# Spreading a per-head reciprocal over partitions through DRAM inside a delta-rule recurrence

## The chip, the cores and the metric

The kernel runs on one core of a Trainium2 chip. The metric is device time in microseconds (us), the median of several runs; before the change it is 1085.88 us (three runs, 1084.61 to 1088.7). Engines: TensorE (PE, with its weight loads as PEld), VectorE (DVE), ScalarE (ACT), GpSimd (POOL) and SyncE (SP), which here only issues DMAs.

## The reference

One layer of a decoder trunk for a sequence of 512 positions and a width of 2048, in float32. After an RMSNorm, one projection gives the streams of two groups. Sixteen heads of 64 channels run a generalised delta rule:

```python
kk = (k * k_k[i]).astype(f32).reshape(B, T, N_HEADS, HEAD_SIZE)
kk = kk / jnp.maximum(jnp.linalg.norm(kk, axis=-1, keepdims=True), KK_EPS)
k = k * (1.0 + (a - 1.0) * k_a[i])
...
sa = jnp.einsum('bhvk,bhk->bhv', S, -kk_t)
S = (S * w_t[:, :, None, :]
     + sa[..., None] * (kk_t * a_t)[:, :, None, :]
     + v_t[..., None] * k_t[:, :, None, :])
y_t = jnp.einsum('bhvk,bhk->bhv', S, r_t)
...
y = head_group_norm(y, ln_w[i], ln_b[i])
bonus = jnp.sum(rh * kh * r_k[i].astype(f32), axis=-1, keepdims=True) * vh
y_rwkv = (y + bonus.reshape(B, T, D_RWKV)).astype(dt) * jax.nn.silu(g_rwkv)
```

The other group takes trailing-window means of 1024 channels. Both are multiplied by gates, projected by w_out and added to x; a gated per-layer embedding and a final RMSNorm follow. What matters here is the second line: the key is divided by its norm, one number for each head and position.

## The kernel before, in words

Channels lie on partitions, time on the free axis. Two reference heads share the 128 partitions, so there are eight "heads" j of 128 channels and 512 positions; each runs as eight chunks of 64 positions. Big products are made from float32 split into a rounded part and a remainder (`wsplit`, `split`: a cast on ScalarE, a subtraction on VectorE), three matmuls for each product.

The middle of the kernel, some 640 us, is a software pipeline over the heads. The order of TensorE's instructions is the order in which they are written (`keep_in_program_order`). A generator `big` holds the stream of large projection matmuls (zk, zr, zv, zg of the coming heads, zb of the pool group), and `pump(n)` puts n of them between two steps of a head, so that TensorE has work while the other engines answer. Weights of that stream come by SP's queue (`raw`, 4 buffers), are cast on ScalarE (`whi`) and split on VectorE (`wlo`). The order on the other engines is found by a list scheduler; `issue_after` puts one instruction behind another on its engine. Every engine, and SP's queue of DMAs, works in the order that results.

Names of a head's steps, in their order of time:

- `prepare_key`: kk = (k k_k)^2 on ScalarE, split into kqh and kql. `norm_key`: two matmuls with a block of ones, `blk`, sum kk over the 64 channels of a head and leave the sum on every partition (PSUM tile pss); a maximum with 1e-24 on VectorE writes it to kk. `scale_key`: reciprocal of kk (128x512, though a column holds only two different numbers), then times k and k_k.
- `decay_and_rate`: decay and rate from small low-rank products.
- `prepare`: the operands ar and bk of the score matmuls; kk enters bk's last product (line 600). Then kp for the bonus.
- `scores`: pm = bk x ar, 32 matmuls, then pbo for the bonus bv.
- `invert`: an inverse of 32x32 triangles by 31 steps on VectorE, spread over the chunks of the head before; the result goes through DRAM (xd) into x1.
- `gather`: y1, two transposes of x1 on VectorE; pq, pmv and px, small matmuls; before them `prepare_key`, `decay_and_rate`, `norm_key` and `scale_key` of the next head.
- `recur`: eight chunks; in each py reads the state, zs is formed on VectorE, pu solves, ScalarE copies to uv, ps updates the state sbd on VectorE. At its end the output ysb is normalised: statistics, and eight scalings of 128x64 (line 866).
- `finish`: transposes of ysb, then yo = scaled output, plus bv, times the gate sg (lines 877, 878), stored by a DMA of ScalarE's queue.

The loop runs `prepare(j + 1)`, `recur(j)` (in it, after the first chunk, `scores(j + 1)` and the steps of `invert(j + 1)`), `gather(j + 1)`. So the key of head j + 2 is normalised in `gather(j + 1)`, and what follows waits for it in `prepare(j + 2)`.

Of the kernel before, what the change touches and what calls it, by code (L numbers as in the profile page):

```python
# [9 lines left out]
F32 = mybir.dt.float32  # L10
# [3 lines left out]
ALU = mybir.AluOpType  # L14

P = 128
T = 512
# [4 lines left out]
NJ = DR // P  # L22
# [12 lines left out]
def trunk_kernel(ctx: ExitStack, tc: tile.TileContext, x, p, norm_g, w_in, mu, w0, w_up, a0, a_up,  # L35
                 k_k, k_a, r_k, ln_w, ln_b, w_pool, pool_scale, w_out, w_ple, w_pg, b_pg, final_g, out):
    nc = tc.nc
    PSUM = bass.MemoryType.PSUM
    x, p, w_in, w_out, w_ple, w_pg = x[0], p[0, 0], w_in[0], w_out[0], w_ple[0], w_pg[0]
    out = out[0]  # L40
# [79 lines left out]
    def dp(o, i):  # L120
        return dprm[:, o + i:o + i + 1]
# [370 lines left out]
    def pump(n):  # L492
        debt[0] += n
        while debt[0] > 0:
            c = next(big, None)
            if c is None:
                debt[0] = 0
                return
            debt[0] -= c
# [12 lines left out]
                assert (nm, j) in zt  # L512
        return zt[nm, j]

    pws, kks, late = {}, {}, [None]

    H1, H2, H3, H4, H5, HE = 6, 12, 20, 8, 13, 40

# [44 lines left out]
    def norm_key(j):  # L563
        kk, kqh, kql = kks[j]
        ps = psM.tile([P, T], F32, name=f"pss{j}", tag="m")
        mm(ps, blk, kqh, start=True, stop=False)
        mm(ps, blk, kql, start=False, stop=True)
        late[0] = nc.vector.tensor_scalar(kk, ps, 1e-24, None, ALU.max)

    def scale_key(j):  # L570
        k_, kk = need("k", j), kks[j][0]
        nc.vector.reciprocal(kk, kk)
        nc.vector.scalar_tensor_tensor(kk, k_, pc("k_k", j), kk, ALU.mult, ALU.mult)
        kks[j] = kk


    def prepare(j):
        k_, r_, v_ = need("k", j), need("r", j), need("v", j)
        pw, ipw, tha = pws.pop(j)
        kk = kks.pop(j)  # L580
        if j + 1 < NJ:
            load_ab(j + 1)


        ar = rw.tile([P, NCH // 2, 4, C], F32, name=f"ar{j}", tag="ar", bufs=2)
        bk = rw.tile([P, NCH // 2, 4, C], F32, name=f"bk{j}", tag="bk")
        k4 = kk.rearrange("p (q c t) -> p q c t", c=2, t=C)
        pw4 = pw.rearrange("p (q c) t -> p q c t", c=2)
        i4 = ipw.rearrange("p (q c) t -> p q c t", c=2)
        kp = rw.tile([P, T], F32, name=f"kp{j}", tag="kp")  # L590
        nc.vector.tensor_scalar(kp, tha, dp(33, j), dp(41, j), ALU.mult, ALU.add)
        nc.vector.tensor_tensor(kp, kp, k_, ALU.mult)
        nc.vector.tensor_scalar(tha, tha, 0.5, 0.5, ALU.mult, ALU.add)
        nc.vector.tensor_tensor(ar[:, :, 0::3, :], r_.rearrange("p (q c t) -> p q c t", c=2, t=C),
                                pw4[:, :, :, 1:C + 1], ALU.mult)
        nc.vector.tensor_tensor(bk[:, :, 0::3, :], kp.rearrange("p (q c t) -> p q c t", c=2, t=C), i4, ALU.mult)
        nc.vector.scalar_tensor_tensor(ar[:, :, 1:3, :], k_.rearrange("p (q c t) -> p q c t", c=2, t=C), dp(89, j),
                                       pw4[:, :, :, 0:C], ALU.mult, ALU.mult)
        nc.vector.tensor_tensor(kk, kk, tha, ALU.mult)
        nc.vector.tensor_tensor(bk[:, :, 1:3, :], k4, i4, ALU.mult)  # L600
        nc.vector.scalar_tensor_tensor(kp, r_, dp(49, j), kp, ALU.mult, ALU.mult)
        kph = rw.tile([P, T], F32R, name=f"kph{j}", tag="t", bufs=4)
        kpl = rw.tile([P, T], F32R, name=f"kpl{j}", tag="t", bufs=4)
        split(kph, kpl, kp)

        bkd = dram.tile([P, NCH * P], F32, name=f"bkd{j}", tag="bkd")
        nc.sync.dma_start(out=bkd, in_=bk.rearrange("p q s c -> p (q s c)"))
        st_[j] = dict(pw=pw, ar=ar, bk=bk, bkd=bkd, v_=v_, kp=(kph, kpl))
# [55 lines left out]
    def invert(j):  # L664
        nb = st_[j].pop("nb")
        xw = rw.tile([P, 8, 32], F32, name=f"xw{j}", tag="xw")
        tm = rw.tile([P, 8, 32], F32, name=f"tm{j}", tag="tm")
        for s in range(31):
            n_, w_ = s // 4 + 1, 31 - s
            xin = i32 if s == 0 else xw  # L670
            nc.vector.tensor_tensor(tm[:, 0:n_, 0:w_], xin[:, 0:n_, s:s + 1].to_broadcast([P, n_, w_]),
                                    nb[s // 16][:, s % 16:s % 16 + 1, s + 1:32].to_broadcast([P, n_, w_]), ALU.mult)
            if s == 0:
                nc.gpsimd.tensor_copy(xw, i32)
            nc.vector.tensor_tensor(xw[:, 0:n_, s + 1:32], xw[:, 0:n_, s + 1:32], tm[:, 0:n_, 0:w_], ALU.add)  # L675
            yield
        xd = dram.tile([2, 2, 8, 8, 4, 32], F32, name=f"xd{j}", tag="xd")
        for q in range(4):
            nc.sync.dma_start(out=xd[:, :, :, :, q, :].rearrange("a b u i c -> (a b u) i c"),
                              in_=xw[32 * q:32 * q + 32])  # L680
        x1 = rw.tile([P, 8, C], F32, name=f"x1{j}", tag="x1", bufs=2)
        nc.gpsimd.memset(x1, 0.0)
        for par in range(2):
            pb = 64 * (1 - par)
            for b in range(2):
                nc.sync.dma_start(out=x1[pb + 32 * b:pb + 32 * b + 32, :, 32 * b:32 * b + 32],
                                  in_=xd[par, b].rearrange("u i q c -> (i q) u c"))

        st_[j]["x1"] = x1


    def gather(j):
        d = st_[j]
        v_, mt = d.pop("v_"), d["mt"]
        if j + 1 < NJ:
            prepare_key(j + 1)
            decay_and_rate(j + 1)

        uv = rw.tile([P, NCH, P], F32, name=f"uv{j}", tag="uv")
# [11 lines left out]
        pump(H4)  # L711

        d.update(uv=uv)
        if j + 1 < NJ:
            norm_key(j + 1)
        pump(H5)
        pump(HX)

# [6 lines left out]

        y1 = rw.tile([P, 8, 32], F32, name=f"y1{j}", tag="tm")

        with tc.issue_after(late[0].ins):
            yt = [nc.vector.transpose(y1[pb:pb + 32], x1[pb:pb + 32, :, 0:32]) for pb in (0, 64)]
        if j + 1 < NJ:  # L730
            with tc.issue_after(yt[0].ins), tc.issue_after(yt[1].ins), tc.issue_after((normed or yt)[-1].ins):
                scale_key(j + 1)
        ps3 = psM.tile([P, 8, 32], F32, name=f"pq2{j}", tag="m")
        units(lambda u, par, pb: mm(ps3[pb + 32:pb + 64, u, :],
# [20 lines left out]
        d["mv"] = mv  # L755
        pump(H1)
        if pending:
            pending.pop()()
        pump(H1)


    def recur(j, work, between):
# [17 lines left out]
        for ch in range(NCH):  # L780
# [27 lines left out]
                    nc.scalar.copy(uv[pb:pb + 64, ch, hc], psu[hc, hc])  # L808
            step()
            pump(HC2)  # L810
            if ch < NCH - 1:
                pss = psS.tile([P, T], F32, name=f"ps{j}_{ch}", tag="s")
                mm(pss[:, 0:P], bkn[:, ch, :], uv[:, ch, :], start=True, stop=True)
                for h in range(2):
                    hc = slice(64 * h, 64 * h + 64)
                    with tc.high_priority(offset=HP):
                        if ch == 0:
                            lead[0] = nc.vector.tensor_scalar(nxt[hc, hc], pss[hc, hc], pcc[hc], None, ALU.mult)
                        else:
                            lead[0] = nc.vector.scalar_tensor_tensor(nxt[hc, hc], pss[hc, hc], pcc[hc], s0p[hc, :],  # L820
                                                                     ALU.mult, ALU.add)
                s0p = rw.tile([P, C], F32, name=f"s0p{j}_{ch}", tag="s0p", bufs=2)
                pcn = pw[:, ch + 1, C:C + 1]
                if ch < NCH - 2:
                    for h in range(2):
                        hc = slice(64 * h, 64 * h + 64)
                        nc.gpsimd.tensor_scalar(s0p[hc, :], nxt[hc, hc], pcn[hc], None, ALU.mult)  # L827
            if ch == NCH - 1:
                for c0 in range(0, NCH, 4):
# [10 lines left out]
                    for pr in range(2):  # L840
                        yr = slice(64 * pr, 64 * pr + 64)
                        nc.scalar.copy(ysb[yr, c0 // 2:c0 // 2 + 2, :], py4[yr, pr::2, :])
            step()
            if ch == 0:
                between()
            else:
                pump(HC3)
# [14 lines left out]
        nc.vector.tensor_scalar(ve8, mvr[:, :, 1:2], 64e-5, None, ALU.add)  # L862
        nt8 = rw.tile([P, 8, 1], F32, name=f"nt8{j}", tag="nt8")
        rsqrt(rs8, ve8, nt8)
        for i in range(8):
            last = nc.vector.tensor_scalar(y8[:, i, :], y8[:, i, :], mvr[:, i, 0:1], rs8[:, i, :],
                                           ALU.subtract, ALU.mult)
        normed.append(last)

        def finish():  # L870
            sg = need("g", j)
            ps = psM.tile([P, T], F32, name=f"pyt{j}", tag="m")
            for tt in range(NT):
                tr(ps[:, tt * P:(tt + 1) * P], ysb[:, tt, :], ident)
            yo = rw.tile([P, T], F32, name=f"yo{j}", tag="t", bufs=4)
            nc.scalar.activation(yo, ps, AF.Identity, scale=dp(57, j), bias=dp(65, j))
            nc.vector.tensor_tensor(yo, yo, bv, ALU.add)
            nc.vector.tensor_tensor(yo, yo, sg, ALU.mult)
            nc.scalar.dma_start(out=yd[j], in_=yo)

        pending.append(finish)

    HC, HT, HX = (6, 9, 9), 130, 13
    HS, HN = 5, 2
    HP = 1000
    pending, normed = [], []
    need("k", 0)
    need("r", 0)
    prepare_key(0)
# [11 lines left out]
    for j in range(NJ):  # L901
# [10 lines left out]
                                    in_=p[256 * h:256 * h + 256, :].rearrange("(t p) q -> p t q", p=P))  # L912
        if j + 1 < NJ:
            prepare(j + 1)
        recur(j, invert(j + 1) if j + 1 < NJ else iter(()), between)
        if j + 1 < NJ:
            gather(j + 1)
    pump(HE)
    pending.pop()()
    s2a.close()  # L920
    psB = ctx.enter_context(tc.tile_pool(name="psB", bufs=3, space=PSUM))
    lp = ctx.enter_context(tc.tile_pool(name="lp", bufs=1))
# [271 lines left out]
```

## Time and profile before

| what | value |
|---|---|
| median of three runs | 1085.88 us (1084.61 to 1088.7) |
| the profiled execution, whole | 1087.06 us |
| its span, first to last instruction | 1085.3 us |
| TensorE busy, weight loads | 97%, 80% |
| VectorE, ScalarE, GpSimd busy | 66%, 41%, 7% |
| mean granted TensorE clock | 0.996 of full |
| DMA, mean | 135 GB/s |

Busy shares are means over a start of some 50 us, the heads up to about 715 us, the output projection to about 910 us and the embedding gate. Matmuls overlap in the records, so that TensorE can show as busy while its next instruction starts a little late; the start times tell more than the busy time.

### The profile page before, as it was taken

How to read it: one execution, taken by the hardware profiler on the slowest of the kernel's cores; microseconds unless marked ns; L12 is line 12 of the kernel's file. 1: busy time of each engine (PE TensorE's matmuls, PEld its weight loads, DVE VectorE, ACT ScalarE, POOL GpSimd, SP SyncE). 2: the span in 40 equal slices, each digit the busy share in tenths (PEclk: the TensorE clock that was granted, in tenths of full speed). 3: DMA queues.
4: the chain of work that ended last, by engine and by line, in shares of the span. 5: the costliest groups of instructions: out<-in, count | busy, mean ns of one | idle time of the engine just before them, and what ended most of it. 6: DMA issues, size and time to landing. Idle time of an engine off the chain costs nothing.

```text
span 1085.3 us, 17105 instructions
## 1 busy us (share of the span) xinstructions
PE 1057.8 (97%) x5996; PEld 873.7 (80%) x5996; DVE 714.9 (66%) x1851; ACT 441.3 (41%) x901; POOL 70.9 (7%) x180
## 2 busy tenths in 40 slices
PE   5999999999999999999999999999999999999996
PEld 4888878888888887887888788888888888888885
DVE  6676968878779779688887966464432424445366
ACT  7633535335336244353353344543222222333337
POOL 2100010010110100100101101000000000000000
PEclk9999999999999999999999999999999999999999
DMA  7444443442533533433435343774434428354534
GB/s 234 112 120 113 135 115 86 114 123 74 156 93 110 143 95 100 117 87 107 115 95 152 99 127 104 244 238 152 166 126 142 168 97 263 129 180 150 178 99 156
DMA packets 212916, 146.94 MB, mean 135 GB/s; under 512 B 68085, under 2 KB 173150, under 8 KB 212830
## 3 DMA queue, kind: packets, MB, share of 16 engines
q1 hardware_dynamic: 192126, 112.28, 35.9%
q10 hardware_dynamic: 20704, 33.56, 9.5%
q8 instruction: 47, 0.77, 0.3%
q14 instruction: 39, 0.32, 0.1%
HBM read 122.21 MB, written 23.07 MB: 134 GB/s over the span
## 4 chain that ended last, share of the span: by engine, by line
PE 76%; DVE 4%; DMA 1%; ACT 1%; issue 0%; SPq 0%; ACTq 0%; DVEq 0%
PE acc_o L157 16%; PE acc_g L157 16%; PE zb L157 13%; PE zg L157 5%; PE zv L157 5%; PE zr L157 5%; PE zk L157 4%; PE pple L157 2%; PE py L157 2%; PE pu L157 1%; PE pm L157 1%; DMA n<-nd 1%; PE pp L157 1%; PE ps L157 1%; PE pmv L157 1%; PE px L1015 1%
## 5 line engine op out<-in xcount | busy, mean ns | idle before, releaser
L133 DVE TENSOR_TENSOR wlo_g<-raw_g,whi_g 128x512 fp32r<-128x512 f32 x84 | 57.1, 685 | 76.0 <-ACT whi_g L132 76.0
L157 PE MATMUL zb<-hhi,whi_b 128*128 128x512 f32 x256 | 106.0, 414 | 0.0
L133 DVE TENSOR_TENSOR wlo_o<-raw_o,whi_o 128x512 fp32r<-128x512 f32 x64 | 43.9, 690 | 91.4 <-ACT whi_o L132 91.4
L157 PE MATMUL zb<-hhi,wlo_b 128*128 128x512 f32 x256 | 100.4, 392 | 0.0
L157 PE MATMUL acc_o<-whi_o,ylo 128*128 128x512 f32 x256 | 100.2, 391 | 0.0
L157 PE MATMUL acc_o<-whi_o,yhi 128*128 128x512 f32 x256 | 99.9, 390 | 0.0
L157 PE MATMUL zb<-hlo,whi_b 128*128 128x512 f32 x256 | 99.8, 390 | 0.0
L157 PE MATMUL acc_o<-wlo_o,yhi 128*128 128x512 f32 x256 | 99.7, 390 | 0.0
L132 ACT CAST whi_g<-raw_g 128x512 fp32r<-128x512 f32 x84 | 52.0, 621 | 106.4 <-PE acc_g L157 59.4
L157 PE MATMUL acc_g<-whi_g,x2hi 128*128 128x512 f32 x208 | 81.2, 391 | 0.0
L157 PE MATMUL acc_g<-wlo_g,x2hi 128*128 128x512 f32 x208 | 81.0, 389 | 0.0
L157 PE MATMUL acc_g<-whi_g,x2lo 128*128 128x512 f32 x208 | 80.6, 389 | 0.0
L132 ACT CAST whi_o<-raw_o 128x512 fp32r<-128x512 f32 x64 | 39.9, 623 | 97.0 <-PE acc_o L157 96.7
L827 POOL TENSOR_SCALAR s0p<-sbd,pw 64x64 f32<-64x64 f32 x96 | 54.5, 568 | 338.6 <-DVE sbd L820 251.0
L132 ACT CAST whi_b<-raw_b 128x512 fp32r<-128x512 f32 x64 | 39.7, 621 | 85.4 <-PE zb L157 28.8
L133 DVE TENSOR_TENSOR wlo_b<-raw_b,whi_b 128x512 fp32r<-128x512 f32 x64 | 43.7, 684 | 28.0 <-ACT whi_b L132 27.6
L157 PEld LDWEIGHTS zb<-hhi,wlo_b 128*128 128x128 f32 x256 | 48.0, 188 | 10.9
L675 DVE TENSOR_TENSOR xw<-xw,tm 128x60 f32<-128x60 f32 (+24 forms) x248 | 52.1, 210 | 7.0
L157 PEld LDWEIGHTS acc_o<-wlo_o,yhi 128*128 128x128 f32 x256 | 48.1, 188 | 10.0
L157 PEld LDWEIGHTS acc_o<-whi_o,ylo 128*128 128x128 f32 x256 | 48.1, 188 | 9.8
L157 PEld LDWEIGHTS acc_o<-whi_o,yhi 128*128 128x128 f32 x256 | 48.1, 188 | 9.7
L157 PEld LDWEIGHTS zb<-hhi,whi_b 128*128 128x128 f32 x256 | 48.2, 188 | 8.3
(283 smaller groups left out, 2532.0 us busy)
## 6 DMA issues: line engine op xcount, KB each, us to landing
raw_b<-in_w_in_dram SPq DMA_DIRECT2D x64, 256.0 KB
raw_o<-in_w_out_dram SPq DMA_DIRECT2D x64, 256.0 KB
raw_g<-in_w_pg_dram SPq DMA_DIRECT2D x64, 256.0 KB
raw_k<-in_w_in_dram SPq DMA_DIRECT2D x32, 256.0 KB
raw_r<-in_w_in_dram SPq DMA_DIRECT2D x32, 256.0 KB
raw_v<-in_w_in_dram SPq DMA_DIRECT2D x32, 256.0 KB
raw_g<-in_w_in_dram SPq DMA_DIRECT2D x32, 256.0 KB
bkd<-bk SPq DMA_DIRECT2D x8, 512.0 KB
```

Of the source, the lines that this page charges most:

```text
L132: nc.scalar.copy(hi, raw)
L133: nc.vector.tensor_tensor(lo, raw, hi.bitcast(F32), ALU.subtract)
L157: i = nc.tensor.matmul(*a, **k)
L675: nc.vector.tensor_tensor(xw[:, 0:n_, s + 1:32], xw[:, 0:n_, s + 1:32], tm[:, 0:n_, 0:w_], ALU.add)
L827: nc.gpsimd.tensor_scalar(s0p[hc, :], nxt[hc, hc], pcn[hc], None, ALU.mult)
L1015: nc.tensor.transpose(pt[:, tt * P:(tt + 1) * P], x2[tt][:, i * P:(i + 1) * P], ident)
```

## The change

For the heads from 1 on the reciprocal is taken once for each head and position. After the sum over channels, `norm_key` copies pss to kk on ScalarE, writes one row for each of the two heads to DRAM (nrd, 2x512) and reads it back as 128x8 (nr). A new step `spread_norm` takes maximum and reciprocal of that tile on VectorE, writes it to DRAM (ird) and reads it back, each row broadcast over 64 partitions, into kk. `scale_key` then only multiplies. All five DMAs go by SP's queue. Head 0 keeps the reciprocal on the whole tile.

Moved are: `prepare_key` and `norm_key` of heads 2 to 7, out of `gather` into the recurrence two heads earlier (chunks 4 and 5), those of head 1 stay in `gather(0)`; `spread_norm` stands in `gather`, behind the last read of x1; the y1 transposes no longer stand behind the maximum; the eight scalings of the output come after them; kp's last product, the bonus sum and the gate (`gate_out`) come behind bk's last product in `prepare`.

```diff
--- before.py
+++ after.py
@@ -512,7 +512,7 @@
                 assert (nm, j) in zt
         return zt[nm, j]
 
-    pws, kks, late = {}, {}, [None]
+    pws, kks, nrs, read = {}, {}, {}, []
 
     H1, H2, H3, H4, H5, HE = 6, 12, 20, 8, 13, 40
 
@@ -565,11 +565,28 @@
         ps = psM.tile([P, T], F32, name=f"pss{j}", tag="m")
         mm(ps, blk, kqh, start=True, stop=False)
         mm(ps, blk, kql, start=False, stop=True)
-        late[0] = nc.vector.tensor_scalar(kk, ps, 1e-24, None, ALU.max)
+        if j == 0:
+            nc.vector.tensor_scalar(kk, ps, 1e-24, None, ALU.max)
+            nc.vector.reciprocal(kk, kk)
+            return
+        nc.scalar.copy(kk, ps)
+        nrd = dram.tile([2, T], F32, name=f"nrd{j}", tag="nrd")
+        nc.sync.dma_start(out=nrd, in_=kk[0::64, :])
+        nr = rw.tile([P, 8], F32, name=f"nr{j}", tag="nr")
+        nc.sync.dma_start(out=nr, in_=nrd.rearrange("h (p e) -> (h p) e", e=8))
+        nrs[j] = nr
+
+    def spread_norm(j):
+        nr, kk = nrs.pop(j), kks[j][0]
+        nc.vector.tensor_scalar(nr, nr, 1e-24, None, ALU.max)
+        nc.vector.reciprocal(nr, nr)
+        ird = dram.tile([2, T], F32, name=f"ird{j}", tag="ird")
+        nc.sync.dma_start(out=ird.rearrange("h (p e) -> (h p) e", e=8), in_=nr)
+        for h in range(2):
+            nc.sync.dma_start(out=kk[64 * h:64 * h + 64], in_=ird[h:h + 1].to_broadcast([64, T]))
 
     def scale_key(j):
         k_, kk = need("k", j), kks[j][0]
-        nc.vector.reciprocal(kk, kk)
         nc.vector.scalar_tensor_tensor(kk, k_, pc("k_k", j), kk, ALU.mult, ALU.mult)
         kks[j] = kk
 
@@ -597,8 +614,11 @@
         nc.vector.scalar_tensor_tensor(ar[:, :, 1:3, :], k_.rearrange("p (q c t) -> p q c t", c=2, t=C), dp(89, j),
                                        pw4[:, :, :, 0:C], ALU.mult, ALU.mult)
         nc.vector.tensor_tensor(kk, kk, tha, ALU.mult)
-        nc.vector.tensor_tensor(bk[:, :, 1:3, :], k4, i4, ALU.mult)
-        nc.vector.scalar_tensor_tensor(kp, r_, dp(49, j), kp, ALU.mult, ALU.mult)
+        made = nc.vector.tensor_tensor(bk[:, :, 1:3, :], k4, i4, ALU.mult)
+        with tc.issue_after(made.ins):
+            nc.vector.scalar_tensor_tensor(kp, r_, dp(49, j), kp, ALU.mult, ALU.mult)
+            if gates:
+                gates.pop()()
         kph = rw.tile([P, T], F32R, name=f"kph{j}", tag="t", bufs=4)
         kpl = rw.tile([P, T], F32R, name=f"kpl{j}", tag="t", bufs=4)
         split(kph, kpl, kp)
@@ -683,8 +703,8 @@
         for par in range(2):
             pb = 64 * (1 - par)
             for b in range(2):
-                nc.sync.dma_start(out=x1[pb + 32 * b:pb + 32 * b + 32, :, 32 * b:32 * b + 32],
-                                  in_=xd[par, b].rearrange("u i q c -> (i q) u c"))
+                read.append(nc.sync.dma_start(out=x1[pb + 32 * b:pb + 32 * b + 32, :, 32 * b:32 * b + 32],
+                                              in_=xd[par, b].rearrange("u i q c -> (i q) u c")))
 
         st_[j]["x1"] = x1
 
@@ -693,7 +713,8 @@
         d = st_[j]
         v_, mt = d.pop("v_"), d["mt"]
         if j + 1 < NJ:
-            prepare_key(j + 1)
+            if j == 0:
+                prepare_key(1)
             decay_and_rate(j + 1)
 
         uv = rw.tile([P, NCH, P], F32, name=f"uv{j}", tag="uv")
@@ -711,8 +732,11 @@
         pump(H4)
 
         d.update(uv=uv)
+        if j == 0:
+            norm_key(1)
         if j + 1 < NJ:
-            norm_key(j + 1)
+            with tc.issue_after(read[-1].ins):
+                spread_norm(j + 1)
         pump(H5)
         pump(HX)
 
@@ -725,10 +749,11 @@
 
         y1 = rw.tile([P, 8, 32], F32, name=f"y1{j}", tag="tm")
 
-        with tc.issue_after(late[0].ins):
-            yt = [nc.vector.transpose(y1[pb:pb + 32], x1[pb:pb + 32, :, 0:32]) for pb in (0, 64)]
-        if j + 1 < NJ:
-            with tc.issue_after(yt[0].ins), tc.issue_after(yt[1].ins), tc.issue_after((normed or yt)[-1].ins):
+        yt = [nc.vector.transpose(y1[pb:pb + 32], x1[pb:pb + 32, :, 0:32]) for pb in (0, 64)]
+        with tc.issue_after(yt[0].ins), tc.issue_after(yt[1].ins):
+            if normed:
+                normed.pop()()
+            if j + 1 < NJ:
                 scale_key(j + 1)
         ps3 = psM.tile([P, 8, 32], F32, name=f"pq2{j}", tag="m")
         units(lambda u, par, pb: mm(ps3[pb + 32:pb + 64, u, :],
@@ -755,7 +780,7 @@
         d["mv"] = mv
         pump(H1)
         if pending:
-            pending.pop()()
+            gates.append(pending.pop()())
         pump(H1)
 
 
@@ -808,6 +833,8 @@
                     nc.scalar.copy(uv[pb:pb + 64, ch, hc], psu[hc, hc])
             step()
             pump(HC2)
+            if j + 2 < NJ and ch == 5:
+                norm_key(j + 2)
             if ch < NCH - 1:
                 pss = psS.tile([P, T], F32, name=f"ps{j}_{ch}", tag="s")
                 mm(pss[:, 0:P], bkn[:, ch, :], uv[:, ch, :], start=True, stop=True)
@@ -841,6 +868,8 @@
                         yr = slice(64 * pr, 64 * pr + 64)
                         nc.scalar.copy(ysb[yr, c0 // 2:c0 // 2 + 2, :], py4[yr, pr::2, :])
             step()
+            if j + 2 < NJ and ch == 4:
+                prepare_key(j + 2)
             if ch == 0:
                 between()
             else:
@@ -862,10 +891,17 @@
         nc.vector.tensor_scalar(ve8, mvr[:, :, 1:2], 64e-5, None, ALU.add)
         nt8 = rw.tile([P, 8, 1], F32, name=f"nt8{j}", tag="nt8")
         rsqrt(rs8, ve8, nt8)
-        for i in range(8):
-            last = nc.vector.tensor_scalar(y8[:, i, :], y8[:, i, :], mvr[:, i, 0:1], rs8[:, i, :],
-                                           ALU.subtract, ALU.mult)
-        normed.append(last)
+
+        def scale():
+            for i in range(8):
+                last = nc.vector.tensor_scalar(y8[:, i, :], y8[:, i, :], mvr[:, i, 0:1], rs8[:, i, :],
+                                               ALU.subtract, ALU.mult)
+            return last
+
+        if j + 1 < NJ:
+            normed.append(scale)
+        else:
+            scale()
 
         def finish():
             sg = need("g", j)
@@ -874,16 +910,20 @@
                 tr(ps[:, tt * P:(tt + 1) * P], ysb[:, tt, :], ident)
             yo = rw.tile([P, T], F32, name=f"yo{j}", tag="t", bufs=4)
             nc.scalar.activation(yo, ps, AF.Identity, scale=dp(57, j), bias=dp(65, j))
-            nc.vector.tensor_tensor(yo, yo, bv, ALU.add)
-            nc.vector.tensor_tensor(yo, yo, sg, ALU.mult)
-            nc.scalar.dma_start(out=yd[j], in_=yo)
+
+            def gate_out():
+                nc.vector.tensor_tensor(yo, yo, bv, ALU.add)
+                nc.vector.tensor_tensor(yo, yo, sg, ALU.mult)
+                nc.scalar.dma_start(out=yd[j], in_=yo)
+
+            return gate_out
 
         pending.append(finish)
 
     HC, HT, HX = (6, 9, 9), 130, 13
     HS, HN = 5, 2
     HP = 1000
-    pending, normed = [], []
+    pending, normed, gates = [], [], []
     need("k", 0)
     need("r", 0)
     prepare_key(0)
@@ -912,11 +952,13 @@
                                     in_=p[256 * h:256 * h + 256, :].rearrange("(t p) q -> p t q", p=P))
         if j + 1 < NJ:
             prepare(j + 1)
+        elif gates:
+            gates.pop()()
         recur(j, invert(j + 1) if j + 1 < NJ else iter(()), between)
         if j + 1 < NJ:
             gather(j + 1)
     pump(HE)
-    pending.pop()()
+    pending.pop()()()
     s2a.close()
     psB = ctx.enter_context(tc.tile_pool(name="psB", bufs=3, space=PSUM))
     lp = ctx.enter_context(tc.tile_pool(name="lp", bufs=1))
```

## Rows read from the trace of the kernel before

**Rows 1.** the page's part 1: busy time, share of the span, instructions of each engine

```profile
...
PE 1057.8 (97%) x5996; PEld 873.7 (80%) x5996; DVE 714.9 (66%) x1851; ACT 441.3 (41%) x901; POOL 70.9 (7%) x180
```

**Rows 2.** what TensorE waited for: total us, times, longest us

```profile
...
PE pm L157 <- DVE bk L600: 3.1, 2, 2.0
...
PE pq L157 <- DVE y L729: 1.7, 2, 0.8
...
PE py L157 <- DVE sbd L820: 0.8, 3, 0.4
...
PE pu L157 <- DVE zs L794: 0.7, 2, 0.4
```

**Rows 3.** TensorE's timeline: start us, us, instruction, idle time before and releaser

```profile
...
427.70 3.01 PE L157 MATMUL pm<-ar,bk 64*128 64x128 f32 x32 [2.04 <-DVE bk L600]
...
432.06 0.40 PE L157 MATMUL zk<-hlo,whi_k 128*128 128x512 f32 x1
432.29 0.40 PE L157 MATMUL zk<-hhi,wlo_k 128*128 128x512 f32 x1
...
489.43 0.69 PE L157 MATMUL pq<-y,mt 32*32 32x32 f32 x30 [0.83 <-DVE y L729]
...
502.94 1.27 PE L157 MATMUL pm<-ar,bk 64*128 64x128 f32 x18 [1.09 <-DVE bk L600]
...
578.01 2.06 PE L157 MATMUL pm<-ar,bk 64*128 64x128 f32 x32
...
580.80 0.39 PE L157 MATMUL zg<-hlo,whi_g 128*128 128x512 f32 x1
```

**Rows 4.** stretches: us, busy of each engine (instructions), PEclk, DMA share, GB/s

```profile
...
427.50:431.00 3.50, 3.30 (x33) 3.07 (x34) 3.09 (x7) 0.00 (x0) 0.00 (x0) 0.66 0.69 231
...
434.00:440.00 6.00, 6.00 (x31) 5.01 (x30) 2.01 (x5) 1.65 (x4) 1.26 (x2) 1.00 0.24 72
```

**Rows 5.** VectorE's groups by line: busy us, mean ns, idle before

```profile
...
L572 DVE RECIPROCAL kk<-kk 128x512 f32<-128x512 f32 x8 | 26.7, 3334 | 0.0
...
L601 DVE SCALAR_TENSOR_TENSOR kp<-sr,dprm,kp 128x512 f32<-128x512 f32 x8 | 6.1, 758 | 0.0
...
L877 DVE TENSOR_TENSOR yo<-yo,bv 128x512 f32<-128x512 f32 x8 | 5.5, 684 | 0.8 <-ACT yo L876 0.8
...
L568 DVE TENSOR_SCALAR kk<-pss 128x512 f32<-128x512 f32 x8 | 5.5, 684 | 0.0
...
L138 DVE TENSOR_TENSOR kql<-kk,kqh 128x512 fp32r<-128x512 f32 x8 | 5.3, 666 | 0.7 <-ACT kqh L137 0.7
...
L1094 DVE RECIPROCAL frs<-frs 128x1 f32<-128x1 f32 x4 | 0.7, 164 | 1.2 <-ACT frs L1088 0.8 <-ACT frs L1090 0.4
```

**Rows 6.** VectorE's timeline before pm of heads 5 and 6

```profile
...
426.97 0.68 DVE L600 TENSOR_TENSOR bk<-kk,ipw 128x512 f32<-128x512 f32 x1
...
488.96 0.42 DVE L729 STREAM_TRANSPOSE y<-x 32x256 f32<-32x256 f32 x1
...
494.10 0.75 DVE L573 SCALAR_TENSOR_TENSOR kk<-sk,prm,kk 128x512 f32<-128x512 f32 x1
...
502.22 0.68 DVE L600 TENSOR_TENSOR bk<-kk,ipw 128x512 f32<-128x512 f32 x1
```

**Rows 7.** SP's queue of DMAs in the stage of head 6 (with its waits)

```profile
...
476.88 1.17 SPq L679 DMA_DIRECT2D xd<-xw  x1
479.81 0.83 SPq L686 DMA_DIRECT2D x<-xd  x2
...
483.41 1.00 SPq L686 DMA_DIRECT2D x<-xd  x2
...
489.01 12.41 SPq L129 DMA_DIRECT2D raw_r<-in_w_in_dram  x4
```

**Rows 8.** ScalarE: one group by line, one row of its timeline

```profile
...
L754 ACT COPY mv<-pmv 128x512 f32<-128x512 f32 x8 | 4.7, 586 | 0.1
...
501.71 0.62 ACT L132 CAST whi_r<-raw_r 128x512 fp32r<-128x512 f32 x1 [1.49 <-issue]
```

## The prediction, made before the result was known

> **What bounds the kernel now.** I read the engine totals first. TensorE is busy for 1057.8 of the 1085.3 us [rows 1], so a change that leaves every matmul in place can only win what TensorE waits for. A busy digit hides waits shorter than a matmul's own length, so the second view is the list of what TensorE waited for. In the eight heads, where the change lies, it names four things [rows 2]: the score matmuls pm for the scaled key bk (3.1 us in two waits), the small solve pq for the transposed y1 (1.7 us in two), and five short waits in the recurrence, py for the state (0.8) and pu for zs (0.7). The other waits of that list are at the start of the kernel, which is untouched.
>
> The timeline shows where. pm of head 5 stands idle for 2.04 us at 427.70, pm of head 6 for 1.09 us at 502.94, one pq for 0.83 us at 489.43 [rows 3]; the second pq wait is the rest of 1.7. After the longest of them TensorE is also slower: the granted clock is 0.66 of full in 427.5 to 431 and 1.00 again in 434 to 440 [rows 4], so it went to the 1.2 GHz level and came back. What that costs is read from the same 35 matmuls at either level: from the first pm to the second matmul of the stream behind it takes 432.06 - 427.70 = 4.36 us there and 580.80 - 578.01 = 2.79 us a head later [rows 3], so 1.57 us.
>
> Behind both pm waits stands VectorE. Between the scaling of the key (494.10) and bk (502.22 to 502.90) it has hardly a pause, and in the head before bk ends at 427.65, as pm starts [rows 6]. So in this stage, and only here, VectorE's queue sets TensorE's time. In the other heads bk ends in time and nothing is gained.
>
> **The change, part by part, for head j+1.**
>
> *Reciprocal.* The 128x512 reciprocal takes 3.33 us on VectorE, eight times [rows 5]. It goes for seven heads (head 0 keeps it). The 128x512 maximum before it, 0.68 us, goes too [rows 5]; a ScalarE copy out of PSUM takes its place, 0.59 us by the copy of the same shape [rows 8], on an engine that is 41% busy [rows 1]. In their place come a maximum and a reciprocal on 128x8. The trace has no 128x8 reciprocal; below it lies the 128x1 one at 0.16 us, above it 3.33 us [rows 5]; in proportion to columns it is 0.16 + 7/511 x 3.17 = 0.2 us, and the maximum about as much. VectorE over the whole kernel: 7 x (3.33 + 0.68 - 0.4) = 25 us less. Little of that is time, since it had cover nearly everywhere.
>
> *Order on VectorE.* Moved behind bk: the bonus sum and gate (two of 0.68 us; [rows 5] shows the first, the second has its shape) and kp's last product (0.76 us). Moved into the recurrence: the split kql (0.67 us, [rows 5]) with its square, cast and two matmuls. The eight scalings of the normalised output now come after the y1 transposes. Ahead of bk the queue is therefore shorter by 3.33 + 0.68 - 0.4 + 1.37 + 0.76 + 0.67 = 6.4 us, if nothing is idle. bk of head 6 would end at 502.90 - 6.4 = 496.5 and TensorE was free for pm at 502.94 - 1.09 = 501.85: cover of 5.3 us. For head 5 it is 421.3 against 425.66: 4.4 us. Both pm waits go, and with the longer one the slow clock behind it.
>
> *y1.* Before, the transposes stand behind the maximum, and between the first and the second came scalings; the second one starts at 488.96 [rows 6], though the read of x1 was issued by 484.41 [rows 7]. Now they come first. What bounds them is the landing of x1: the write of xd ended its issue at 478.05 and the read that waits for it went out at 479.81 [rows 7], so so about 1.8 us for such a small transfer, and x1 is there by 486.2 to 487. Both pq waits go, 1.7 us.
>
> *The detour through DRAM.* Five DMAs a head, all on SP's queue, none before: two for the norms (written, read back as 128x8) in the recurrence, then the write of the reciprocals and two broadcasts behind the x1 reads. The first two have from chunk 5 to the end of the head, some 20 us. The other three lie on a chain: x1 reads issued (484.41), write, landing, two broadcast reads, landing, scaling. At best 0.2 for the arithmetic, 0.5 issue, 1.8 landing, 1.0 issue (as the two x1 reads, [rows 7]), 1.8 landing: 5.3 us, so 489.7. At worst each of the two steps also stands behind one weight load that waits for its buffer on the same queue; four such loads take 12.41 us [rows 7], about 3 us each: 495.7. The scaling was at 494.10 before; without reciprocal, maximum and kql VectorE would reach it 3.33 + 0.68 + 0.67 - 0.4 = 4.3 us sooner, at 489.8. VectorE keeps order, so a late landing holds all that is queued behind the scaling: weight splits, then bk. At best it waits for nothing, at worst for 5.9 us, of which 5.3 (4.4 in head 5) are covered by the shorter queue. I take no cost, since both weight loads have to stand in the way at once; the bounds are 0 and 1.5 us a head. For SP the added waits delay weight loads by a few us; the first raw_r load goes out at 489.01 and is first read at 501.71 [rows 7, 8], so 10 us of cover.
>
> *Head 1* has all four hops inside one stage, some 9 us in a row, where the reciprocal took 3.3 us. Its key has to be there some 5 us later than that; I take nothing, bound 3 us once.
>
> *In the recurrence* six heads get 0.67 us more on VectorE at chunk 4 and 1.9 us more on ScalarE. If kql stands in front of a step of the chain, TensorE waits up to 0.67 us, 6 x 0.67 = 4.0 us. The nearest rows are the five waits for zs and the state, 1.5 us in all [rows 2], so 0.3 us each, over eight heads that are full of such VectorE work; collisions are rare, and I take 0.4 us for the six heads.
>
> **Sum.** 3.1 + 1.7 + 1.6 = 6.4 us off, 0.4 on: 6.0 us. Against the profiled execution, 1087.06 us in all (span 1085.3), that is 1081.1; this execution was 1.2 us over the median of the runs shown, so for the median 1085.88 - 6.0 = **1079.9 us**, 0.55% less. A change under 0.5% (5.4 us) can't be told from none here, so the forecast lies just past that line.
>
> **Rivals.**
>
> *A, waits go as above: 0.58.* 1077 to 1083; the gain is capped by the waits, not by the 25 us of VectorE. Of this 0.42 below 1080.45 and 0.16 above.
>
> *B, the waits move: 0.25.* kql, square and copy hit the recurrence in every head (4.0 us), or the slow clock was not part of the median run (1.6 us). 1085.88 - 6.0 + 4.0 = 1084; with both 1085.5, and with 0.5 us a head for a late landing besides, 1089. For it: the waits for state and zs show that the chain has little to spare. Against: they are short.
>
> *C, slower: the broadcast comes too late: 0.10.* If VectorE idles 8 us at the scaling, where 5.3 are covered, pm waits 2.7 us in seven heads, and each wait brings the slow clock (1.6 us): 7 x 4.3 = 30 us, in place of the 6.4 us of now: 1085.88 + 30 - 6.4 = 1110; in half of the heads 1095. It decides from a landing later than 495.1, so 10.7 us after the x1 reads. For it: SP is a queue in order, and weight loads wait in it. The Trainium skill (DMA: Bandwidth & Descriptors, Anatomy of one DMA) also speaks against the change: it gives each DMA about 2 us of fixed cost whatever its size, most of it the receipt of the last write, worst for HBM. The 1.8 us between xd and x1 agrees; by the page's 2 us the two hops would end 0.3 us later and the sum stays.
>
> *D, more than the named waits: 0.07.* The queue that VectorE works off 6 us sooner also frees the recurrence's first chunks: 1.5 us more, and small waits inside busy time. About 1076 to 1078. [...] The trace shows matmuls of 0.39 us that start 0.23 us apart (432.06 and 432.29, [rows 3]), so waits below 0.16 us are indeed not seen.
>
> **Chances.** Faster by over 0.5%: 0.42 of A and D, 0.49. Within: 0.16 of A and 0.20 of B, 0.36. Slower: 0.05 of B and C, 0.15. The range takes A, D and most of B: 1075 to 1088; A's own is 1077 to 1083.
>
> **What would show it.** Right: no pm or pq in TensorE's waits, clock 1.00 throughout the heads, ScalarE up 4 us and VectorE down 25. The detour is harmless if VectorE's idle time before the scaling (line of the key's k_k product) is under 5 us a head. Wrong: pm still waits, for bk behind a broadcast (C); new or longer py and pu waits near chunks 4 to 6 (B); or the waits go and the time stays, in which case the profiled waits were not those of the timed runs.

## The result and the profile after

The change makes the kernel slower: 1088.7 us (median of 13 runs, 1087.27 to 1089.97) against 1084.66 us (median of 13 runs on the same chip), a ratio of 1.0025 with a 95% interval of 1.0016 to 1.0034. That is under the 0.5% named in the prediction as the line to no change, but it goes the other way, clear of the noise, and 1088.7 lies just outside the range of 1075 to 1088.

Engine totals of the changed kernel (before: [rows 1]):

```profile
PE 1058.3 (97%) x5996; PEld 873.1 (80%) x5996; DVE 694.4 (64%) x1851; ACT 443.8 (41%) x908; POOL 75.6 (7%) x180
```

VectorE has 20.5 us less work, ScalarE 2.5 more, in the direction that was forecast but less of it (25 and 4). TensorE's work is the same. What it waited for, in the changed kernel (us in all, times, longest; before: [rows 2]):

```profile
...
PE px L157 <- issue: 4.5, 1, 4.5
...
PE py L157 <- DVE sbd L847: 2.5, 5, 1.0
```

The waits of pm and pq are gone from the list, 4.8 us of waiting, as forecast. In their place stand one wait of 4.5 us at px, the last small product of `gather` in head 0, and longer waits of py for the state (2.5 us, before 0.8). The second differs from execution to execution: in two more of the kernel before py waits 1.7 and 1.6 us, in one more of the changed kernel 1.2. So the change can't be blamed for it from these profiles.

Where the time went is read best from the start of pm, once a head (from TensorE's timeline, us from the start of the span):

| profiled execution | pm head 0 | pm head 1 | pm head 7 | end | 0 to 1 | 1 to 7 | 7 to end |
|---|---|---|---|---|---|---|---|
| before, first profile | 75.89 | 132.45 | 578.01 | 1085.3 | 56.6 | 445.6 | 507.3 |
| changed | 75.43 | 138.36 | 579.63 | 1087.7 | 62.9 | 441.3 | 508.1 |

So heads 1 to 7 have won 4.3 us and the one stage between pm of head 0 and pm of head 1 has lost 6.4. That stage holds `gather(0)` and `prepare(1)`. The loss is nearly the same in every execution (56.5 and 56.6 us in two more of the kernel before, 62.3 in one more of the changed kernel); the gain is not (445.2 and 443.9 against 439.2).

VectorE's timeline of the changed kernel there:

```profile
...
112.90 0.29 DVE L526 TENSOR_TENSOR us<-ur,us 64x128 fp32r<-64x128 f32 x1
116.51 0.44 DVE L752 STREAM_TRANSPOSE y<-x 32x256 f32<-32x256 f32 x1 [3.32 <-DMA x<-xd]
...
117.44 1.23 DVE L534 TENSOR_TENSOR_SCAN sig<-seg,sig 128x512 f32<-128x512 f32 x1
...
123.35 0.27 DVE L526 TENSOR_TENSOR as<-ar,as 64x128 fp32r<-64x128 f32 x1
```

And ScalarE's (rows with q after ACT are DMAs that it issues):

```profile
...
118.70 0.63 ACT L539 ACTIVATE pw<-sig 128x512 f32<-128x512 f32 x1 [5.83 <-DVE sig L534]
...
123.70 0.52 ACTq L354 DMA_DIRECT2D ar<-in_a_up_dram  x1
124.27 0.62 ACT L132 CAST whi_b<-raw_b 128x512 fp32r<-128x512 f32 x1 [1.96 <-DVE as L526]
...
125.50 0.74 ACT L766 COPY q<-pq 32x256 f32<-32x256 f32 x2
```

The same steps in the kernel before, from the timeline of all its engines:

```profile
...
113.41 1.23 DVE L534 TENSOR_TENSOR_SCAN sig<-seg,sig 128x512 f32<-128x512 f32 x1
...
114.67 0.64 ACT L539 ACTIVATE pw<-sig 128x512 f32<-128x512 f32 x1 [1.34 <-DVE sig L534]
...
116.81 0.90 DVE L729 STREAM_TRANSPOSE y<-x 32x256 f32<-32x256 f32 x2
...
121.32 0.74 ACT L741 COPY q<-pq 32x256 f32<-32x256 f32 x2 [1.61 <-issue]
...
122.23 0.69 PE L157 MATMUL px<-x,q 32*32 32x32 f32 x32
...
128.71 1.12 ACTq L354 DMA_DIRECT2D ar<-in_a_up_dram  x2
```

The first y1 transpose, no longer held behind the maximum, has been put ahead of the decay's scan. It waits 3.32 us for x1 to land, the scan stands behind it, and ScalarE, whose next instruction reads the scan, stands still for 5.83 us with all that is queued behind it. A second stop follows: the load of the next head's a_up weights (`load_ab`, line 354) is issued by ScalarE's queue, has to wait until VectorE's `as` has read the old ones, and now stands ahead of the copies out of pq. px needs these copies:

```profile
...
126.34 1.07 PE L157 MATMUL px<-x,q 32*32 32x32 f32 x32 [4.47 <-issue]
```

The granted clock after that wait, in the changed kernel (third column from the right; engines' busy time ahead of it; before: [rows 4]):

```profile
...
127.00:131.00 4.00, 4.00 (x25) 3.19 (x21) 0.69 (x1) 1.46 (x4) 0.40 (x1) 0.57 0.34 102
131.00:138.00 7.00, 7.00 (x34) 5.82 (x33) 5.24 (x9) 2.28 (x5) 1.17 (x2) 1.00 0.49 164
```

So the 1.2 GHz level, which the change removed behind pm of head 5, came back in head 0: in 127 to 131 a matmul follows the last after 0.43 us where 0.23 is usual.

### The profile page after: what moved, and what is told of

It is laid out like the page before. It is cut to its first block, busy times and chain, and to the rows that moved or that the text cites. A ratio compares the mean times of both kernels' runs of the same rounds, so it can differ in the third digit from the quotient of the medians.

```text
span 1087.7 us, 17173 instructions
## 1 busy us (share of the span) xinstructions
PE 1058.3 (97%) x5996; PEld 873.1 (80%) x5996; DVE 694.4 (64%) x1851; ACT 443.8 (41%) x908; POOL 75.6 (7%) x180
## 4 chain that ended last, share of the span: by engine, by line
PE 86%; DVE 5%; DMA 3%; issue 2%; ACT 2%; SPq 1%; ACTq 0%; DVEq 0%
PE acc_o L157 16%; PE acc_g L157 16%; PE zb L157 14%; PE zv L157 8%; PE zr L157 7%; PE zk L157 6%; PE zg L157 6%; DMA n<-nd 3%; PE pple L157 2%; PE py L157 2%; PE pu L157 1%; PE pm L157 1%; PE ps L157 1%; PE pp L157 1%; PE px L1057 1%
```

## The experiments

All ratios are against the kernel before, run in turns on the same chip. The experiments ran on three chips, on which the kernel before had medians of 1087.37, 1086.57 and 1086.31 us, so ratios are compared and not times. Two theories stood at first. *Order*: the transposes ahead of the scan make the loss. *Detour*: the four DMA hops of head 1, which have no recurrence to hide in, make it.

**The transposes behind the scan, in head 0.**

```diff
+        scans[j] = nc.vector.tensor_tensor_scan(sig, seg, sig, 0.0, ALU.mult, ALU.add)
...
+        with tc.issue_after(scans[1 if j == 0 else 0].ins):
+            yt = [nc.vector.transpose(y1[pb:pb + 32], x1[pb:pb + 32, :, 0:32]) for pb in (0, 64)]
```

> The changed kernel with one order put back: in head 0 the two y1 transposes stand behind the decay's scan on VectorE, not ahead of it. Theory (order): TensorE's wait of 4.5 us at px in head 0 and the 1.4 us of slow clock behind it are gone, and nothing else moves; 1088.7 - 5.9 = about 1083, so 0.1 to 0.2% under the kernel before. Rival (detour): the four DMA hops of head 1 in one stage hold the engines, the transposes are innocent; px still waits 4 us or more, 1088 or above.

Measured: 1.0013 (0.9999 to 1.0028), by the two ratios some 1.3 us better than the change, not 5.9, and not clear of the noise. The scan is on time and px still waits, 2.5 us with the slow clock behind it (granted 0.50 in 124 to 129). VectorE's, then ScalarE's timeline of this run:

```profile
...
121.13 0.27 DVE L527 TENSOR_TENSOR as<-ar,as 64x128 fp32r<-64x128 f32 x1
```

```profile
...
114.39 0.63 ACT L540 ACTIVATE pw<-sig 128x512 f32<-128x512 f32 x1 [1.76 <-DVE sig L535]
...
121.48 0.47 ACTq L354 DMA_DIRECT2D ar<-in_a_up_dram  x1
121.99 0.62 ACT L132 CAST whi_b<-raw_b 128x512 fp32r<-128x512 f32 x1 [4.00 <-PE pmv L157]
...
123.22 0.74 ACT L768 COPY q<-pq 32x256 f32<-32x256 f32 x2
```

pw starts 4.3 us sooner than in the changed kernel, the copies out of pq only 2.3: the load of ar goes out at 121.48, when `as` ends at 121.40, and ScalarE idles 4.00 us. (The view blames pmv, which had long ended.) In the kernel before, that load stands behind the copies (128.71, above).

**Head 1's key on the whole tile, no hop in the first stage.**

```diff
-        if j == 0:
+        if j <= 1:
             nc.vector.tensor_scalar(kk, ps, 1e-24, None, ALU.max)
             nc.vector.reciprocal(kk, kk)
             return
```

(`spread_norm` is then called from head 2 on.)

> The changed kernel, but head 1, like head 0, takes the reciprocal on the whole 128x512 tile: no DMA hop is left in the first stage. The transposes stay free. Theory (order): the first transpose still stands ahead of the scan and waits for x1, so px in head 0 waits 4 to 5 us as now; 1088 to 1089. Rival (detour): that wait is gone, about 1083.

Measured: 0.9986 (0.9971 to 1.0001). TensorE's waits:

```profile
...
PE px L157 <- issue: 1.7, 1, 1.7
```

ScalarE's timeline:

```profile
...
117.66 0.64 ACT L539 ACTIVATE pw<-sig 128x512 f32<-128x512 f32 x1 [5.17 <-DVE sig L534]
...
122.29 0.74 ACT L767 COPY q<-pq 32x256 f32<-32x256 f32 x2
...
130.87 1.13 ACTq L354 DMA_DIRECT2D ar<-in_a_up_dram  x2
```

Between the two theories: px still waits, but 1.7 us, with no slow clock (1.00 in 123 to 128). Without the detour the scheduler places the loads of ar behind the copies again, so only the transposes' stop is left.

**The detour alone** (the kernel before with the new key path; scalings, bonus, gate unmoved; transposes behind the small reciprocal, in head 0 behind the scan) and **the moves alone** (the reverse: the key as before).

> The kernel before with the detour through DRAM alone: key of heads 2 to 7 in the recurrence, reciprocal on 128x8, broadcast from DRAM; scalings, bonus and gate stay where they were, the transposes stand behind the small reciprocal (in head 0 behind the scan). Theory: VectorE's queue ahead of bk is still shorter by some 4 us, enough for the two pm waits; no long wait in head 0; 1082 to 1084. Rival (the moved scalings, bonus and gate carry the gain): pm still waits in heads 5 and 6, 1085 or above.

> The kernel before with the moves alone: transposes free, scalings behind them, kp's last product, bonus and gate behind bk; the key is normalised as before, no DMA is added. Theory (order): the first transpose of head 0 stands ahead of the scan as in the changed kernel, px waits 4 us or more and the clock drops: 1088 to 1091. Rival (detour): without DMAs no such wait; 1081 to 1084.

Measured: 1.0024 (1.0011 to 1.0036) and 1.0041 (1.0023 to 1.0060): neither half gains, and from pm of head 1 to pm of head 7 they take 446.7 and 448.8 us, more than the kernel before (445.6). TensorE's waits, the detour alone:

```profile
...
PE py L157 <- DVE sbd L844: 3.9, 5, 2.2
...
PE px L157 <- issue: 3.2, 1, 3.2
PE pq L157 <- DVE y L751: 1.3, 2, 1.0
```

The moves alone:

```profile
...
PE py L157 <- DVE sbd L824: 5.0, 5, 1.7
...
PE px L157 <- issue: 3.0, 2, 1.9
PE pyt L161 <- DVE ysb L872: 1.4, 2, 0.7
```

With the moves alone px of head 0 waits 1.9 us, much as in the run without hops (1.7), so the time came out as expected but not by the wait of 4 us or more that was to make it. With the detour alone px waits 3.2 us although the transposes stand behind the scan: the load of ar is again ahead of the copies (issued at 123.04, the copies at 124.36). pm waits no more, so the shorter queue does that by itself; pq waits again, as in the kernel before, where the transposes are not free either. In both, py waits longer for the state than in the changed kernel; what makes these waits was not tried in these two.

**Both orders put back in head 0, the detour whole.** The transposes behind the scan, and the loads for head 2 behind the copies:

```diff
+        if j == 1:
+            with tc.issue_after(mvc[0].ins):
+                load_ab(2)
+        elif j + 1 < NJ:
             load_ab(j + 1)
```

> The changed kernel again, beside the others of this call on one chip: 0.2 to 0.4% over the kernel before, px in head 0 waiting 4 to 5 us, as in its first profile.

> The changed kernel with two orders put back in head 0: the y1 transposes behind the scan on VectorE, and the four loads of the next low-rank weights on ScalarE's queue behind the copies out of pq and pmv, not ahead of them. The detour through DRAM stays whole. Theory (two orders): in the run with the transposes behind the scan alone, ScalarE's queue still stood 3.3 us at the load of ar, which waits for VectorE to be done with the old ar, and px waited 2.5 us with 2.4 us of slow clock; with both orders back px waits under 0.5 us, the clock stays up, and the time is some 5 us under that run: 0.2 to 0.4% under the kernel before. Rival (detour): the hops of head 1 hold something else and px still waits 2 us or more; no gain over the kernel before.

Measured: the changed kernel 1.0015 (1.0005 to 1.0025), with px waiting 3.2 us, less than the 4 to 5 expected; this one 1.0016 (1.0008 to 1.0025). px waits no more, and nothing is gained. TensorE's waits:

```profile
...
PE py L157 <- DVE mt L656: 2.3, 1, 2.3
PE pm L157 <- DVE bk L621: 1.6, 1, 1.6
```

VectorE's timeline, then SP's queue, of this run:

```profile
...
123.94 0.17 DVE L582 TENSOR_SCALAR nr<-nr 128x8 f32<-128x8 f32 x1 [2.56 <-DMA nr<-nrd]
124.15 0.20 DVE L583 RECIPROCAL nr<-nr 128x8 f32<-128x8 f32 x1
...
130.20 0.75 DVE L591 SCALAR_TENSOR_TENSOR kk<-sk,prm,kk 128x512 f32<-128x512 f32 x1 [5.25 <-DMA kk<-ird]
```

```profile
...
116.86 0.55 SPq L575 DMA_DIRECT2D nrd<-kk  x1
...
119.94 0.45 SPq L577 DMA_DIRECT2D nr<-nrd  x1
...
124.38 0.34 SPq L585 DMA_DIRECT2D ird<-nr  x1
126.21 1.15 SPq L587 DMA_DIRECT2D kk<-ird  x2
```

With TensorE on time, the detour of head 1 is late by itself: 13.3 us from the first write (116.86) to the scaling (130.20), and VectorE stands idle for 2.56 and 5.25 us of them. pm waits for bk, then py for a mask product behind it. So the first stage has three things that hold it: the transposes, the load of ar, the four hops. With the first two gone the third is seen, and it alone costs as much as all three: from pm of head 0 to pm of head 2 this version takes 135.8 us, the changed kernel 136.1 and the kernel before 130.6.

**The inverse begun two steps later** (HS 7 for 5; key steps in chunks 5 and 6), on top of the last.

> The one before with the inverse begun two steps later in the recurrence (first step after hop 7 for 5, key steps of the head after in chunks 5 and 6 for 4 and 5). Theory: the first inverse step stands in VectorE's queue ahead of the state update and waits for its operand n from DRAM, the longer the sooner pm runs; begun later, VectorE's wait for n goes from 17 us in all to under 6, the waits of py for the state at the start of the inverse go, and the time falls by another 1.5 to 3 us. Rival: those waits come from the weight splits in front of the update, not from n; py waits as before, no change.

Measured: 1.0022 (1.0013 to 1.0032), no gain. VectorE's wait for n falls as expected, py's waits for the state with it (from 1.5 us to 0.3):

```profile
DVE tm L695 <- DMA n<-nd: 3.7, 1, 3.7
```

But px waits 1.4 us in two places, as it would if x1 came too late, and the first stage still has pm waiting 1.8 and py 2.0 us. So py's waits for the state hang on where the inverse begins, and most likely on n; two steps are too many.

**The kernel before without the reciprocal in heads 1 to 7** (a constant in place of the norm's inverse there).

> The kernel before without the reciprocal in heads 1 to 7: the maximum is replaced by a multiply-add that writes a small constant, so the key is not normalised there; all else and every order that the text fixes is as before. It bounds what taking the 3.3 us off VectorE can give when nothing is added. By the prediction: pm and pq waits and the slow clock behind pm gone, 4 to 6 us under the kernel before. Rival: TensorE's waits move to the next place where VectorE is late (py for the state, behind the wait for n), and the gain is 0 to 2 us.

Measured: 0.9989 (0.9981 to 0.9998), 1.2 us, where 4 to 6 were expected from the prediction. TensorE's waits:

```profile
...
PE py L157 <- DVE sbd L821: 2.0, 3, 0.9
PE pu L157 <- ACT x L752: 1.9, 1, 1.9
PE pq L157 <- DVE y L730: 1.6, 2, 0.8
```

pm waits no more. pq waits as before, since the transposes still stand behind the scalings; py waits 2.0 us (0.8, 1.7 and 1.6 in the three profiles of the kernel before); and the order in head 0 came out so that pu waits 1.9 us for the copies into x1. So this version, too, lost time in the first stage, 58.7 us from pm of head 0 to pm of head 1 against 56.6, while from there to head 7 it takes 441.3, which is 2.6 to 4.3 us less than the profiles of the kernel before. The 1.2 us are therefore no clean bound on what the shorter VectorE queue is worth in the heads.

**What the changed heads are worth: no detour in head 1, and the transposes of head 0 behind the scan.** The edits of the first two experiments together; the second run begins the inverse one step later besides (HS 6 for 5).

> The changed kernel with head 1's key taken on the whole tile as before (no detour inside the first stage) and, in head 0, the transposes behind the scan; heads 2 to 7 are as changed. Theory (the loss is made in the first stage alone, by two things: the transposes ahead of the scan, and a detour of four hops that has no time there): px, pm and py of the first stage wait under 0.5 us each, the clock stays up, and the time is 0.3% (3 us) under the kernel before, which keeps small waits for the state. Rival (the heads 2 to 7 have lost as much as they won): no more than 0.15% under.

> The one before, with the inverse begun one step later in the recurrence (after hop 6 for 5). Theory: VectorE's wait for n falls from 16 us in all to under 9, with it py's waits for the state at the start of the inverse; x1 comes later by less than the pq copies can bear; 0.4 to 0.5% under the kernel before. Rival: x1 is late, pq or px wait in its place, no better than the one without it.

Measured: 0.9955 (0.9942 to 0.9967), 4.9 us under the kernel before, and 0.9942 (0.9929 to 0.9956), 6.3 us; medians 1080.97 and 1078.93 against 1086.31. By these ratios both beat both kernels; between the two of them the intervals overlap. From pm of head 0 to pm of head 1 both take 56.5 us, as before the change; from there to head 7, 441.5 and 438.0. The stretch of the first stage in the second of them (TensorE's busy time is the first number after the length; the clock is 1.00):

```profile
...
113.00:138.00 25.00, 25.00 (x222) 20.62 (x220) 22.57 (x37) 11.91 (x25) 2.10 (x3) 1.00 0.46 130
```

What TensorE waits for state, in the first and in the second:

```profile
...
PE py L157 <- DVE sbd L850: 2.4, 3, 1.4
```

```profile
...
PE py L157 <- DVE sbd L850: 0.2, 1, 0.2
```

VectorE's wait for n fell less than expected, from 17.6 to 15.0 us, so the expectation of under 9 was wrong; py's wait for the state fell all the same.

With the first of the two, the runs above fill a square of the two edits. Each field has the ratio to the kernel before and the time from pm of head 0 to pm of head 2 in the profiled execution (130.6, 129.9 and 130.3 us in three of the kernel before):

| | four hops in head 1 | head 1 on the whole tile |
|---|---|---|
| transposes ahead of the scan | 1.0025 and 1.0015; 136.1 and 135.4 us | 0.9986; 131.4 us |
| transposes behind the scan | 1.0013; 136.1 us | 0.9955; 129.9 us |

While the hops are there, the place of the transposes is worth 0.1% at most; without the hops it is worth 0.3%. Taking out the hops, and with them the order of `as` and the load of ar that they bring, is worth 0.3 to 0.4% by itself and 0.6% with the transposes in place (each ratio has an interval of 0.1 to 0.15% to either side). So the hops of head 1 are the larger part of the loss.

**The kernel before, looked at twice more**, to see what its waits are from execution to execution.

> The kernel before, a second look. Theory: of the waits that the prediction removed, the two of pq and the one of pm in head 6 are in every execution, the long one of head 5 with its slow clock is not always: an execution near 1084.5 us has pm waiting under 2 us in all and full clock in the heads. Rival: both pm waits and the slow clock are there in every execution.

> The kernel before, a third look, for the same question: how much pm, pq and the slow clock behind pm vary from execution to execution. Theory: pm's total differs by over 1 us between the three looks and goes with the whole time.

Measured: 1087.83 and 1085.05 us. pm waits 3.1 us and pq 1.6 in both, as in the first profile (3.1 and 1.7): these waits are in every execution seen, and both theories fell, which had pm's wait differ. The slow clock is not in every one: in 427.5 to 431 the granted clock was 0.66, then 0.52, and in the third look

```profile
427.50:431.00 3.50, 3.50 (x34) 3.00 (x31) 3.50 (x8) 0.00 (x0) 0.00 (x0) 1.00 0.70 233
```

after the same wait of 2.0 us. The third look is also the shortest.

## Why the prediction was wrong

*Which waits go.* Right. pm and pq wait no more, VectorE's reciprocal on 128x8 takes 0.20 us as estimated, and in heads 2 to 7 the three hops behind the x1 reads cost nearly nothing: VectorE idled 3.3 us before the scaling in all, 2.4 of it in head 1.

```profile
...
L590 DVE SCALAR_TENSOR_TENSOR kk<-sk,prm,kk 128x512 f32<-128x512 f32 x8 | 5.9, 740 | 3.3 <-DMA kk<-ird 3.3
...
L582 DVE RECIPROCAL nr<-nr 128x8 f32<-128x8 f32 x7 | 1.4, 202 | 0.2
```

*y1.* This is the first step that failed. "Now they come first. What bounds them is the landing of x1" is true of the transposes, and I asked what that does for pq. I didn't ask what stands behind a transpose that waits in VectorE's queue. In heads 1 to 6 the scan had been done by then (head 7 has none); in head 0 it had not, so the free transpose went ahead of it and held scan, ScalarE, copies and px in turn. The old text's tie to the maximum, which looked like a delay, kept it out of the way.

*Head 1.* The second, and the larger of the two. "I take nothing, bound 3 us once" was put on some 9 us for four hops, from the 1.8 us between xd and x1. They took 11.2 us in the changed kernel and, with TensorE on time, 13.3 us: the read of nr in pieces of 32 bytes landed 3.6 us after its issue ended (120.39 to 123.94), the broadcast 2.8 us (127.36 to 130.20). pm and py waited 3.9 us for it. The term put at nothing was some 5 us: that much is lost from pm of head 0 to pm of head 2 when only the hops are left. The bound of 3 us was too low as well. Besides, with the later key the list scheduler placed `as` and the load of ar in another order, which no row of before could show; without the hops the old order is back. The page that the prediction set against the change (the Trainium skill, DMA: Bandwidth & Descriptors, Anatomy of one DMA) gives about 2 us of fixed cost, in a section on DMAs that GpSimd issues, which these are not. The write of ird came in under that (1.5 us from the end of its issue, 124.72, to the broadcast at 126.21), the two reads into SBUF took more.

*The sum.* 6.0 us were to be won. Heads 1 to 7 won 4.3, with 1.6 of slow clock among what went; the third look at the kernel before has no slow clock and takes 443.9 us from head 1 to head 7, so against it only 2.6 were won. With the changed kernel's second profile (439.2 us) it is 4.7 to 6.3, so the heads won somewhere between 2.6 and 6.3 us. Rival B said that waits move. py's waits for the state nearly go when the inverse begins later (0.2 and 0.3 us); that the change made them longer is not shown, since they differ as much between executions of one kernel. Rival C was wrong: no broadcast of heads 2 to 7 came late enough. What the sum left out, the 6.4 us of the first stage, is larger than what it held.

The last versions show that the mechanism was sound in heads 2 to 7: with the first stage as it was, the change there is worth 0.45%, and 0.58% with the inverse one step later, where 0.55% was forecast. How much of the last step the kernel before would gain by itself was not tried, so the 0.58% can't be put down to the change alone.

## What to carry to other kernels

A tie that holds an instruction back may be what keeps a waiting instruction out of the queue's front: when it is cut, ask in every iteration, the first above all, what stands behind that instruction on its engine, DMA issues included. A detour through DRAM that the loop hides has no cover in the iteration that starts the pipeline; leave that one on the old path. And where several engines reach a point at about the same time, taking one stop away may gain little until the others are gone too (the transposes here: 0.1% with the hops, 0.3% without), so test them together before calling any of them harmless.

## What was not expected of the hardware

After the same idle time of 2.0 us at the same place TensorE's granted clock fell to the 1.2 GHz level in two of three executions of the same kernel (0.66 and 0.52 in 427.5 to 431) and stayed at 2.4 GHz in the third (1.00). A 4 KB read from DRAM into 128 partitions, in pieces of 32 bytes, landed 3.6 us after its issue ended (120.39 to 123.94), twice the 1.8 us of the write of xd, and in the other profiles of head 1's detour after 1.6 to 3.9 us. Weight loads of 256 KB stand beside it on the same queue; whether they or the small pieces make it late was not tried.
